# Fourier mixing on operands folded over tokens and channels, with the background tasks moved earlier

## The chip, the cores and the metric

The kernel runs on one core of one Trainium2 chip. Time is device microseconds (us) of one execution; the value used is the median of the runs. The core has the tensor engine (PE, with its weight loads as PEld), the vector engine (DVE), the scalar engine (ACT), GpSimd (POOL, idle here) and the queue that starts transfers (SP). Each engine works through its own instructions in a fixed order and waits on semaphores for the others.

## The reference

A two-layer backbone for 256 tokens `x` of 2048 channels and 256 context tokens `ctx`, all in fp32. Layer 0 multiplies the modulated, normed input by one wide matrix, feeds retention and Fourier mixing, gates both, and projects back. Layer 1 is a gated short convolution.

```python
def _fourier(u, fno_w):
    b, L, _ = u.shape
    ug = u.reshape(b, L, G_B, GB_DIM).astype(jnp.float32)
    f = jnp.fft.fft2(ug, axes=(1, 3), norm='ortho').real
    y = jnp.einsum('blgc,gcd->blgd', f.astype(u.dtype), fno_w)
    return y.reshape(b, L, B_WIDTH)
...
    qx, kx, vx, gax, ux, gbx = _split_even(hx @ w_in)
...
    yx = jnp.concatenate([_merge_heads(ret_x, hx.dtype) * jax.nn.silu(gax),
                          _fourier(ux, fno_w) * jax.nn.silu(gbx)], axis=-1) @ w_out
...
def _odd_layer(h, w_in, conv_w, w_out, rows):
    bg, cg, xt, g = jnp.split(h @ w_in, 4, axis=-1)
    y = bg * _conv3(cg * xt, conv_w, rows) * jax.nn.silu(g)
    return y @ w_out
```

Every layer starts with `rmsnorm(x) * (1 + scale) + shift` and ends with `x + gate * y`; scale, shift and gate are rows of `silu(c) @ ada_w + ada_b`. The Fourier part has 8 groups of 256 channels; the transform runs over the 256 tokens and the 256 channels of a group, and its real part is kept.

## The kernel before

Each fp32 operand is held as two parts, hi and lo, and a product is three matmul passes: hi by hi, lo by hi, hi by lo, summed in PSUM. All matmuls go through `mm` (L56). Activations lie channel-major: 8 tiles `hx` of 128 partitions x 2 x (256 hi | 256 lo), and 8 `hc` for the context.

A weight tile is 128x2048 fp32, 1 MB. SP loads it (`load_raw`, L82) into a ring `raw` of three buffers. `split_w` takes it in four quarters of 512: ACT casts the hi part (`whi`, L95), DVE subtracts it for the lo part (`wlo`, L59). Each of these rings has six quarters, so six quarters can be ready ahead of PE. `group_t` makes 256 output columns channel-major from two tiles (64 matmuls for one stream), `group_n` 512 columns token-major from four tiles (96 matmuls, 512 wide), and `group_d` sums the last block of a projection in one bank.

Two kinds of work are threaded through these groups. `bg` pops a background task at every second weight tile, unless `quiet` is set: a 1 MB load of a row block `adaT` into the same `raw` ring, and a DVE reduction with `scb` (L371) into a column of `gv`. There are 64 tasks; `finish_mods` adds a range of `gv` into `mods`, and first pops, one after the other, every task of that range that hasn't been popped. `hook` pops one closure from `stages` after every half weight tile; a closure holds a stage of a retention head (S, o, then the norm: sum `ss`, root on ACT, reciprocal on DVE at L190), or of a Fourier group. A scheduler then fixes the order on each engine.

The phases are: start (norms, first modulation); retention in four pairs `pr` of heads (K, Q, V, then two gates `gA`, ending in `yA`); Fourier mixing; output projection with `w0o` in eight blocks; layer 1 (`w1`, 64 groups); the second projection (`w1o`). Mixing has four rounds of one `group_n` for the product u (`gN`), a `fold` of u over the channel, and two gate groups. A Fourier group is `tables` (12 matmuls `pz` on the group's weights `wr`), `tokens` (18 matmuls `pP`) and `product` (12 matmuls `py`); then `gate` makes `yB`. Its `load` of `wr` goes into a buffer of its own, and is issued ahead of the groups of its round.

In the output projection `project` sets `quiet` for blocks 6 and 7. Of the 64 tasks 20 are popped in retention, 16 in mixing, 12 in the output projection, 16 in layer 1. At `finish_mods(16, 48)`, behind the projection, 48 have been popped. `modulate` then writes `h1` from `x1`: `modt` (L196), a cast, and `h` (L198).

## Time and profile before

| what | us |
|---|---|
| the three runs | 1835.57, 1834.95, 1835.39 |
| median | 1835.39 |
| span of the profiled execution | 1833.4 |
| matmuls (PE) busy | 1792.8 |
| DVE busy | 1202.4 |
| ACT busy | 906.0 |

The span is read from the first to the last instruction of one profiled execution; the runs' times lie 1.6 to 2.2 us above it, and no other time of that execution is given. A row of a group names line, engine, operation, output and input, shape and count, then busy time and mean nanoseconds of one, then the idle time before it and what ended it. A row of a window gives its length, the busy time of PE, PEld, DVE, ACT and POOL with the number of instructions, the granted PE clock (1.00 is full), the share of the DMA engines and GB/s. A row of the chain of waits gives start, duration, engine, tile, line and count. A row of an engine's timeline gives start, duration, engine, line, operation and, in brackets, the idle time ahead with what ended it. A row of the waits says who waited on whom: total, times, longest.

### The profile page before, as it was taken

The numbers are of one execution on the slowest core, as the hardware profiler recorded it, in microseconds if no ns is written. First come the engines' busy times: TensorE is split into PE (matmuls) and PEld (weight loads), VectorE is DVE, ScalarE is ACT, GpSimd is POOL, SyncE is SP. The second block draws the span as 40 slices with busy tenths as digits, with TensorE's granted clock in tenths as the row PEclk, the third lists the DMA queues.
The fourth block names the chain that finished last, engine by engine and source line by source line (L and its number), as shares of the span: only waits on it lengthen the run. The fifth ranks groups of instructions, "written<-read, shape, count | busy, mean of one in ns | idle before, by whom it ended". The sixth has DMA issues, their size and how long they took to land.

```text
span 1833.4 us, 26739 instructions
## 1 busy us (share of the span) xinstructions
PE 1792.8 (98%) x10200; PEld 1541.9 (84%) x10200; DVE 1202.4 (66%) x1862; ACT 906.0 (49%) x1491; POOL 0.2 (0%) x4
## 2 busy tenths in 40 slices
PE   5999999999999999999999999999999999999997
PEld 3667888888888888888978888888888888888887
DVE  5347747557477777777587888666666666665554
ACT  4225626345265554444555555555555555555553
POOL 0000000000000000000000000000000000000000
PEclk8999999999999999999999999999999999999999
DMA  9886445545466676777547877555555555555552
GB/s 389 327 319 246 144 156 184 180 165 186 150 238 250 243 258 229 262 291 287 196 161 253 299 279 288 191 187 197 191 184 191 196 188 185 189 199 186 186 192 105
DMA packets 58449, 400.87 MB, mean 219 GB/s; under 512 B 6480, under 2 KB 6608, under 8 KB 11088
## 3 DMA queue, kind: packets, MB, share of 16 engines
q1 hardware_dynamic: 58320, 399.16, 60.5%
q8 instruction: 80, 1.31, 0.3%
q14 instruction: 49, 0.40, 0.1%
HBM read 397.03 MB, written 2.10 MB: 218 GB/s over the span
## 4 chain that ended last, share of the span: by engine, by line
PE 95%; DVE 2%; ACT 1%; DMA 1%; issue 0%; SPq 0%; DVEq 0%
PE gT L56 70%; PE gN L56 12%; PE gD L56 3%; PE gemv L56 2%; PE pk L56 1%; PE o L56 1%; PE pvc L56 1%; PE pvx L56 1%; PE pP L56 1%; PE S L56 1%; PE pz L56 1%; PE py L56 1%; DMA raw<-w0s 1%; PE pq L56 1%; DMA xT<-xT 0%
## 5 line engine op out<-in xcount | busy, mean ns | idle before, releaser
L95 ACT CAST whi<-raw 128x512 fp32r<-128x512 f32 x1088 | 670.9, 622 | 746.1 <-PE gT L56 535.8
L59 DVE TENSOR_TENSOR wlo<-raw,whi 128x512 fp32r<-128x512 f32 x1088 | 738.3, 690 | 452.4 <-ACT whi L95 436.7
L56 PE MATMUL gT<-h,whi 128*128 128x512 f32 x2048 | 711.3, 392 | 4.2 <-DVE h L198 4.2
L56 PE MATMUL gT<-h,wlo 128*128 128x256 f32 x2048 | 573.2, 280 | 0.0
L56 PEld LDWEIGHTS gT<-h,whi 128*128 128x128 f32 x2048 | 383.6, 187 | 88.8 <-issue 4.5
L56 PEld LDWEIGHTS gT<-h,wlo 128*128 128x128 f32 x2048 | 387.5, 189 | 0.7 <-DVE wlo L59 0.3
L56 PE MATMUL gT<-hx,whi 128*128 128x512 f32 x704 | 254.5, 401 | 1.6 <-ACT v L478 1.6
L56 PE MATMUL gT<-hx,wlo 128*128 128x256 f32 x704 | 197.9, 281 | 0.1
L371 DVE CUSTOM_DVE_ANT_0 raw<-raw,scb 128x2048 f32<-128x2048 f32 x64 | 146.5, 2290 | 48.0 <-DMA raw<-adaT 45.0
L56 PEld LDWEIGHTS gT<-hx,whi 128*128 128x128 f32 x704 | 132.2, 188 | 32.3 <-ACT v L478 2.1
L56 PE MATMUL gT<-y,whi 128*128 128x512 f32 x448 | 155.3, 391 | 0.0
L56 PE MATMUL gN<-whi,hx 128*128 128x512 f32 x448 | 139.3, 392 | 0.0
L56 PEld LDWEIGHTS gT<-hx,wlo 128*128 128x128 f32 x704 | 132.9, 189 | 1.8 <-DVE wlo L59 0.7
L56 PE MATMUL gT<-y,wlo 128*128 128x256 f32 x448 | 125.4, 280 | 0.0
L56 PEld LDWEIGHTS gT<-y,whi 128*128 128x128 f32 x448 | 83.8, 187 | 18.4
L56 PEld LDWEIGHTS gN<-whi,hx 128*128 128x128 f32 x448 | 83.5, 188 | 16.9
L56 PE MATMUL gN<-wlo,hx 128*128 128x512 f32 x224 | 87.3, 390 | 0.0
L56 PEld LDWEIGHTS gT<-y,wlo 128*128 128x128 f32 x448 | 84.7, 189 | 0.0
L56 PE MATMUL gT<-yB,whi 128*128 128x512 f32 x224 | 79.5, 399 | 0.0
L56 PE MATMUL gT<-yA,whi 128*128 128x512 f32 x224 | 79.4, 398 | 0.0
L56 PE MATMUL gT<-yB,wlo 128*128 128x256 f32 x224 | 62.9, 281 | 0.0
L56 PE MATMUL gT<-yA,wlo 128*128 128x256 f32 x224 | 62.9, 281 | 0.0
(233 smaller groups left out, 1792.4 us busy)
## 6 DMA issues: line engine op xcount, KB each, us to landing
raw<-w SPq DMA_DIRECT2D x200, 1024.0 KB, 4.9
raw<-adaT SPq DMA_DIRECT2D x64, 1024.0 KB, 4.9
raw<-ada SPq DMA_DIRECT2D x32, 1024.0 KB, 6.9
raw<-w0o SPq DMA_DIRECT2D x32, 1024.0 KB, 4.9
raw<-w1o SPq DMA_DIRECT2D x32, 1024.0 KB, 4.8
raw<-w0s SPq DMA_DIRECT2D x8, 1024.0 KB, 5.7
xT<-xT SPq DMA_DIRECT2D x4, 512.0 KB, 6.7
cT<-ctxT SPq DMA_DIRECT2D x4, 512.0 KB, 16.2
```

The source lines that it names most:

```text
L56: nc.tensor.matmul(o, l, r, start=start, stop=stop, skip_group_check=True)
L59: nc.vector.tensor_tensor(o, x, hi.bitcast(F32), op=ALU.subtract)
L95: nc.scalar.copy(hi[:], sl)
L371: nc.vector.tensor_tensor_reduce(out=raw[:], in0=raw[:], in1=scb[:], scale=1.0, scalar=0.0, op0=ALU.mult, op1=ALU.add, accum_out=gv[:, j:j ...
```

## The change

Over tokens, `fold_x` makes sums and differences of tokens t and 256 - t from `hx` into new tiles `hf`, all eight in the last retention pair. Over channels, `half.fold` makes sums (`ef`) and differences (in place) of the columns c and 256 - c of the weights of u, two tiles per pair of 512 columns, before they are split. A cosine needs only the even sums and a sine only the odd differences, so each half of u (`u0`, `u1`; bank pair `pu`) takes 16 steps of 6 matmuls. What folding leaves over, token 128 and channel 128, goes through `uacc` (one DVE operation for each 512 columns), two fp32 products with `e0`, and `middle` (48 products 128x8 and one fp32). The gates are computed from `hf` and unfolded by `gate_unfold`.

The work is threaded anew: the 16 steps of `u0` hang on the gate groups 0 to 3, the steps of `u1` together with Fourier groups 0 to 3 on gate groups 4 to 7, and Fourier groups 4 to 7 on the first block of the output projection. The last pair of retention goes K, V, Q, gA. Background tasks come at every weight tile in the first three pairs (28), none from the last pair to the end of mixing, and at every second tile in the projection (12), so `finish_mods(16, 48)` pops eight. `wr` is loaded within `tables`, into a ring it shares.

```diff
+        often = [True]
...
-            if tasks and turn[0]:
+            if tasks and (turn[0] or often[0]):
...
+        hf = [None] * 8
+        xd = const.tile([P, 16], F32, name="xd")
+
+        def fold_x(e):
+            s = rp.tile([P, 2, 256], F32, tag="t2", bufs=5, name="hs")
+            add(s[:], hx[e][:, :, 0:256].bitcast(F32), hx[e][:, :, 256:512].bitcast(F32))
+            eo = rp.tile([P, 2, 256], F32, tag="t2", bufs=5, name="eo")
+            add(eo[:, :, 1:128], s[:, :, 1:128], s[:, :, 255:128:-1])
+            dif(eo[:, :, 129:256], s[:, :, 1:128], s[:, :, 255:128:-1])
+            add(eo[:, :, 0:1], s[:, :, 0:1], s[:, :, 128:129])
+            dif(eo[:, :, 128:129], s[:, :, 0:1], s[:, :, 128:129])
+            hf[e] = act_tile(f"c{e}", f"hf{e}")
+            split_act(hf[e], eo[:])
+            nc.vector.tensor_scalar(xd[:, 2 * e:2 * e + 2].unsqueeze(2), eo[:, :, 128:129], 2.0, None, op0=ALU.mult)
...
+            else:
+                quiet[0] = True
+                k, kc = keys()
+                keep(values())
+                stages += [(lambda e=e: fold_x(e)) for e in range(4)]
+                q = queries()
+                h0, h1 = heads()
+                stages += [h0[0], lambda: fold_x(4), h0[1], lambda: fold_x(5), h0[2], h1[0], lambda: fold_x(6), h1[1]]
...
+            if pr == 3:
+                fold_x(7)
+                h1[2]()
...
+        class half:
+            def __init__(self, hf):
+                self.hf, self.pu, self.raws = hf, None, {}
+            def fold(self, i):
+                raw = load_raw(a["w0u"][self.hf * 8 + i])
+                r = raw[:].rearrange("p (k s c) -> p k s c", k=2, s=2)
+                ef = fp.tile([P, 2, 512], F32, tag="ef", name="ef")
+                add(ef[:], r[:, :, 0, :], r[:, :, 1, :])
+                dif(r[:, :, 0, :], r[:, :, 0, :], r[:, :, 1, :])
+                if i == 0:
+                    self.acc = fp.tile([P, 512], F32, tag="acc", name="uacc")
+                self.raws[i] = (ef, r)
+            def step(self, kc):
+                if self.pu is None:
+                    self.pu = psum("pu")
+                    self.fold(0)
+                i, k2 = kc // 2, kc % 2
+                ef, r = self.raws[i]
+                w = []
+                for src in (ef[:, k2, :], r[:, k2, 0, :]):
+                    hi = wp.tile([P, 512], F32R, tag="whi", bufs=6, name="whi")
+                    lo = wp.tile([P, 512], F32R, tag="wlo", bufs=6, name="wlo")
+                    nc.scalar.copy(hi[:], src)
+                    sub(lo[:], src, hi[:])
+                    w.append((hi[:], lo[:]))
+                if kc == 0:
+                    nc.vector.tensor_scalar(self.acc[:], r[:, k2, 1, :], xd[:, 0:1], None, op0=ALU.mult)
+                else:
+                    nc.vector.scalar_tensor_tensor(self.acc[:], r[:, k2, 1, :], xd[:, kc:kc + 1], self.acc[:],
+                                                   op0=ALU.mult, op1=ALU.add)
+                x = hf[kc // 2]
+                for s in range(2):
+                    c0 = s * 128
+                    mm3(self.pu[:, s, :], (x[:, k2, c0:c0 + 128], x[:, k2, 256 + c0:384 + c0]), w[s], kc == 0,
+                        kc == 15 and s == 0)
+                if k2 and i < 7:
+                    self.fold(i + 1)
+                if kc == 15:
+                    mm(self.pu[:, 1, :], e0[:], self.acc[:], False, True)
+                    self.h = fp.tile([P, 2, 512], F32R, tag="uh", name="uh")
+                    self.l = fp.tile([P, 2, 512], F32R, tag="ul", name="ul")
+                    nc.scalar.copy(self.h[:], self.pu[:])
+                    sub(self.l[:], self.pu[:], self.h[:])
+                    for t in (self.h, self.l):
+                        t0 = t[:, 1, :].rearrange("p (g c) -> p g c", g=4)[:, :, 0:1]
+                        nc.vector.tensor_scalar(t0, t0.bitcast(F32), row0[:], None, op0=ALU.mult)
...
+                wr = fp.tile([P, 512], F32, tag="t2", bufs=4, name="wr")
+                nc.sync.dma_start(wr[:], a["fno"][g].rearrange("p a c -> p (a c)"))
+                wgh = wp.tile([P, 512], F32R, tag="whi", bufs=6, name="wgh")
+                wgl = wp.tile([P, 512], F32R, tag="wlo", bufs=6, name="wgl")
...
-                even, odd, mid = ubox[-1]
+                for t, src in zip(mids, (umh[:, g:g + 1], uml[:, g:g + 1], umh[:, 8 + g:9 + g], uml[:, 8 + g:9 + g])):
+                    nc.vector.tensor_copy(t[:, 0:1], src.bitcast(F32))
+                mh, ml, kh, kl = (t[:] for t in mids)
+                eh, el = u.h[:, 0, j:j + 128], u.l[:, 0, j:j + 128]
+                oh, ol = u.h[:, 1, j:j + 128], u.l[:, 1, j:j + 128]
                 pP = bank("pP")
-                for lc in range(2):
-                    i = 2 * lc + g % 2
-                    mm3(pP[:, 0:256], [t[:, i, :] for t in even],
-                        (th[:, lc, 0:256], tl[:, lc, 0:256]), lc == 0, lc == 1)
-                for lc in range(2):
-                    i = 2 * lc + g % 2
-                    mm3(pP[:, 256:512], [t[:, i, :] for t in odd],
-                        (th[:, lc, 256:512], tl[:, lc, 256:512]), lc == 0, False)
-                    mm3(pP[0:32, 256:512], [t[:, i, :] for t in mid],
-                        (th[:, lc, 0:256], tl[:, lc, 0:256]), False, lc == 1)
+                po = pP[:, 0:256]
+                mm3(po, (eh, el), (th[:, 0:256], tl[:, 0:256]), True, False)
+                mm(po, oh, nt[:], False, False)
+                mm(po, ol, nt[:], False, True)
+                po, p0 = pP[:, 256:512], pP[0:32, 256:512]
+                mm3(po, (oh, ol), (th[:, 256:512], tl[:, 256:512]), True, False)
+                mm3(p0, (mh, ml), (th[:, 0:256], tl[:, 0:256]), False, False)
+                mm(p0, kh, nt[:], False, False)
+                mm(p0, kl, nt[:], False, True)
...
-            def load():
-                wr = got["wr"] = fp.tile([P, 2, 256], F32, tag="wr", bufs=1, name="wr")
-                nc.sync.dma_start(wr[:], a["fno"][g])
...
-        for gp in range(4):
-            g0, g1 = fourier(2 * gp), fourier(2 * gp + 1)
-            g0[0]()
-            stages += [None, last, None, None, g0[1], None, None, None]
-            stages += [None, g0[2], None, g0[3], None, g1[1], g1[2], None]
-            pu, = group_n(w0, iw, [hx])
-            iw += 4
-            ubox.append(fold(pu))
-            g1[0]()
-            tg, = group_t(w0, iw, 2, [hx])
-            iw += 2
-            g0[4](silu_lr(fp, tg, "sgb", 1))
-            tg, = group_t(w0, iw, 2, [hx])
-            iw += 2
-            sgb = silu_lr(fp, tg, "sgb", 1)
-
-            def last(g1=g1, sgb=sgb):
-                g1[3]()
-                g1[4](sgb)
-        stages += [None, last]
...
+        def gate_unfold(g):
+            tg, = group_t(a["w0g"], 2 * g, 2, [hf])
+            s = lr(fp, tg, bufs=4, ring=4)
+            n = fp.tile([P, 2, 256], F32, tag="t2", bufs=4, name="un")
+            add(n[:, :, 0:128], s[:, :, 0:128], s[:, :, 128:256])
+            dif(n[:, :, 128:129], s[:, :, 0:1], s[:, :, 128:129])
+            dif(n[:, :, 129:256], s[:, :, 127:0:-1], s[:, :, 255:128:-1])
+            sgb[g] = fp.tile([P, 2, 256], F32, tag="sgb", bufs=4, name="sgb")
+            nc.scalar.activation(sgb[g][:], n[:], AF.Silu, scale=0.5)
...
+        stages += [(lambda kc=kc: u0.step(kc)) for kc in range(16)]
+        for g in range(4):
+            gate_unfold(g)
+        stages += [both(lambda kc=kc: u1.step(kc), *((middle,) if kc == 0 else ()), gs[kc // 4][kc % 4])
+                   for kc in range(16)]
+        for g in range(4, 8):
+            gate_unfold(g)
+        g4, g5, g6, g7 = gs[4:]
+        g4[0]()
+        g4[1]()
+        stages += [both(g4[2], g5[0], g5[1]), both(g4[3], g5[2], g6[0], g6[1]), both(g5[3], g6[2], g7[0], g7[1]),
+                   both(g6[3], g7[2]), g7[3]]
+        quiet[0] = often[0] = False
```

Three places show how the order moves. The first is PE at the end of retention; `ss` is the last head's sum of squares. Before, the first product for u follows it:

```order
L56 MATMUL gT_4003<-hx7_87,wlo_4084 128x256
L56 MATMUL ss_4119<-sq_4066,ones_72 128x256
L56 MATMUL gN_4168<-whi_4174,hx0_80 128x512 x2
L56 MATMUL gN_4168<-wlo_4175,hx0_80 128x512
L56 MATMUL gN_4168<-whi_4178,hx0_80 128x512 x2
```

In the changed kernel `gT_4300` is the first gate group of mixing, `o` the last head's weighted values:

```order
L56 MATMUL gT_4300<-hf3_3918,wlo_4316 128x256
L56 MATMUL o_4209<-mask_3317,v_3774 128x256 x6
L56 MATMUL ss_4238<-sq_4218,ones_72 128x256
L56 MATMUL pu_4335<-whi_4342,hf0_3819 128x512 x2
L56 MATMUL pu_4335<-wlo_4343,hf0_3819 128x512
L56 MATMUL pu_4335<-whi_4346,hf0_3819 128x512 x2
```

On DVE the changed kernel has these rows there, behind the reciprocal of that head, up to the first operations on a u weight tile (`eo`, `xd` and `hf7` belong to the last `fold_x`, `ot` and `yA7` to the head):

```order
L65 TENSOR_TENSOR eo_4229<-hs_4227 128x2
L68 TENSOR_TENSOR eo_4229<-hs_4227 128x2
L62 TENSOR_TENSOR ot_4243<-o_4209,rstd_4240 128x512
L467 TENSOR_SCALAR xd_1191<-eo_4229 128x2
L62 TENSOR_TENSOR ot_4243<-ot_4243,sga_4225 128x512
L59 TENSOR_TENSOR hf7_4234<-eo_4229,hf7_4234 128x2x256
L59 TENSOR_TENSOR yA7_4249<-ot_4243,yA7_4249 128x2x256
L559 MEMSET e0_4273 128x128
L562 MEMSET row0_4276 128x1
L566 MEMSET zero_4283 128x32
L65 TENSOR_TENSOR ef_4338<-raw_4336 128x1024
L637 TENSOR_SCALAR uacc_4341<-raw_4336,xd_1191 128x512
```

The head's last operations and the last `fold_x` now lie between `ss` and the first weights of u, on the engine that folds them.

The second place is SP at the end of mixing: `raw<-w0o` are weights of the output projection, `raw<-adaT` tasks, `wr` weights of a Fourier group.

```order
L85 DMA raw_5961<-w0g 128x2048
L675 DMA wr_5880<-fno 128x512
L85 DMA raw_6122<-w0o 128x2048
L85 DMA raw_6124<-adaT 128x2048
L85 DMA raw_6296<-w0o 128x2048
L85 DMA raw_6427<-w0o 128x2048
L675 DMA wr_6076<-fno 128x512
L675 DMA wr_6172<-fno 128x512
```

`wr_6076` is group 4's and `wr_6172` group 5's; the loads of groups 4 to 7 stand among those of the output projection, where before they all stood ahead of it.

The third place is SP and DVE at the boundary to layer 1. Before, on SP, from the last weights of the projection on (`xr` is a block of `x`):

```order
L82 DMA raw_7985<-w0o 128x2048
L82 DMA raw_8051<-w0o 128x2048
L685 DMA xr_7850<-xT 128x512
L82 DMA raw_8207<-w1 128x2048
L82 DMA raw_8257<-w1 128x2048
```

The changed kernel on SP:

```order
L85 DMA raw_8061<-w0o 128x2048
L813 DMA xr_7860<-xT 128x512
L85 DMA raw_8142<-adaT 128x2048
L85 DMA raw_8145<-adaT 128x2048
L85 DMA raw_8148<-adaT 128x2048
L85 DMA raw_8151<-adaT 128x2048
L85 DMA raw_8154<-adaT 128x2048
L85 DMA raw_8157<-adaT 128x2048
L85 DMA raw_8160<-adaT 128x2048
L85 DMA raw_8163<-adaT 128x2048
L85 DMA raw_8241<-w1 128x2048
```

And on DVE, where an `ISA` row on `raw` is a reduction (the first of the eight stands further up), `x1_7` the last block of the projection, and `rstd` its norm:

```order
L375 ISA raw_8151,gv_76<-raw_8151,scb_1185 128x2048
L375 ISA gv_76 128x1
L775 SCALAR_TENSOR_TENSOR x1_7_6547<-gD_7862,mods_77,xr_7860 128x256 x2
L375 ISA raw_8154,gv_76<-raw_8154,scb_1185 128x2048
L375 ISA gv_76 128x1
L194 RECIPROCAL rstd_8139<-rstd_8139 128x256
L375 ISA raw_8157,gv_76<-raw_8157,scb_1185 128x2048
L375 ISA gv_76 128x1
L375 ISA raw_8160,gv_76<-raw_8160,scb_1185 128x2048
L375 ISA gv_76 128x1
L375 ISA raw_8163,gv_76<-raw_8163,scb_1185 128x2048
```

The next DVE rows add `gv` into `mods`. Eight loads and eight reductions now stand between the projection and layer 1; before, the first `w1` load followed the projection's.

More of the change, by code (lines that the diff above doesn't have):

```diff
@@ new lines, in body, with mm3, middle @@
+        umh = fp.tile([P, 16], F32R, name="umh")
+        uml = fp.tile([P, 16], F32R, name="uml")
+        ys = yA + [None] * 8
+        def mm3(o, x, y, start, stop):
+            mm(o, x[0], y[0], start, False)
+            mm(o, x[1], y[0], False, False)
+            mm(o, x[0], y[1], False, stop)
+        def middle():
+            pm = bank("pm")
+            for kc in range(16):
+                x = hf[kc // 2]
+                mm3(pm[:, 0:8], (x[:, kc % 2, 0:128], x[:, kc % 2, 256:384]), (dmh[:, kc, :], dml[:, kc, :]),
+                    kc == 0, kc == 15)
+            pr = fp.tile([P, 16, 8], F32, tag="t2", bufs=4, name="pr")
+            mul(pr[:], dm[:], xd[:].unsqueeze(2).to_broadcast([P, 16, 8]))
+            cr = fp.tile([P, 8], F32, name="cr")
+            nc.vector.tensor_reduce(cr[:], pr[:].rearrange("p k g -> p g k"), axis=AX.X, op=ALU.add)
+            nc.vector.tensor_scalar(cr[:], cr[:], 0.5, None, op0=ALU.mult)
+            mm(pm[:, 8:16], e0[:], cr[:], True, True)
+            nc.scalar.copy(umf[:], pm[:, 0:16])
+            nc.scalar.copy(umh[:], umf[:])
+            sub(uml[:], umf[:], umh[:])
@@ new lines, in body, with both, f @@
+        u0, u1 = half(0), half(1)
+        gs = [fourier(g, u0 if g < 4 else u1) for g in range(8)]
+        def both(*fs):
+            def f():
+                for x in fs:
+                    x()
+            return f
+        stages += [(lambda kc=kc: u0.step(kc)) for kc in range(16)]
[5 more added lines that the diff above has]
+            gate_unfold(g)
@@ L692, in body @@
                                        op0=ALU.add, op1=ALU.mult)
[L695 removed]
+        h1 = [act_tile(f"c{e}", f"h1_{e}") for e in range(8)]
         for kc in range(16):
```

182 lines of the change are left out of this document (95 added, 87 removed).

## The prediction

> **What bounds the kernel now.** I read the page's head first, then the mean durations of the two splitting steps, then the stretch in which the change works (windows from 500 to 800 us).
>
> ```profile
> span 1833.4 us, 26739 instructions
> PE 1792.8 (98%) x10200; PEld 1541.9 (84%) x10200; DVE 1202.4 (66%) x1862; ACT 906.0 (49%) x1491; POOL 0.2 (0%) x4
> PE 95%; DVE 2%; ACT 1%; DMA 1%; issue 0%; SPq 0%; DVEq 0%
> ```
> ```profile
> 500.00:600.00 100.00, 100.00 (x541) 86.61 (x540) 76.73 (x113) 57.05 (x95) 0.00 (x0) 1.00 0.68 253
> 600.00:700.00 100.00, 100.00 (x573) 87.55 (x572) 72.70 (x105) 52.41 (x91) 0.00 (x0) 1.00 0.65 238
> 700.00:800.00 100.00, 100.00 (x583) 87.66 (x582) 72.20 (x104) 49.28 (x84) 0.00 (x0) 1.00 0.70 264
> ```
> ```profile
> L59 DVE TENSOR_TENSOR wlo<-raw,whi 128x512 fp32r<-128x512 f32 x1088 | 738.3, 690 | 452.4 <-ACT whi L95 436.7 <-PE gT L56 1.3
> L371 DVE CUSTOM_DVE_ANT_0 raw<-raw,scb 128x2048 f32<-128x2048 f32 x64 | 146.5, 2290 | 48.0 <-DMA raw<-adaT 45.0 <-ACT scb L366 2.7
> L95 ACT CAST whi<-raw 128x512 fp32r<-128x512 f32 x1088 | 670.9, 622 | 746.1 <-PE gT L56 535.8 <-PE gN L56 113.7 <-DVE wlo L59 36.5
> ```
>
> The tensor engine (PE) is busy in all of each of the three windows, at clock 1.00, and 95% of the chain that ended last is PE. The casts on ACT wait for PE (535.8 us), not PE for them. So a matmul taken out saves its time in full, and nothing else saves anything, as long as PE stays fed. The engine nearest to the bound is DVE: 72 to 77% there. The question of this change is what PE loses in waits where it now has 98%.
>
> **What is removed and added on PE.** These pieces of the chain of waits give start, duration and count; the last row is from PE's timeline.
>
> ```profile
> 238.18 1.73 PE S L56 x8
> ...
> 518.90 5.55 PE gT L56 x32
> 524.45 0.43 PE ss L56 x2
> 524.88 21.79 PE gN L56 x96
> ...
> 681.76 2.13 PE pP L56 x18
> ```
> ```profile
> 142.49 0.95 PE L56 MATMUL gemv<-cols,gs 128*128 128x2 f32 x8
> ```
>
> A matmul 512 wide takes 21.79/96 = 0.227 us. The u product falls from 4 x 96 = 384 of them to 192: -43.6. The token transforms fall from 18 to 13 per group at 2.13/18 = 0.118, 40 in all: -4.7. The middle channel's 48 products 128x8 have no row. Their floor is that row's 0.95/8 = 0.119, their ceiling a 512-wide 0.227; so narrow, they lie at the floor: +5.7 (to 10.9). The products of e0 are plain fp32, as ss is: that one instruction, 256 wide, shows as two passes of together 0.43 (S has 1.73/8 a pass as well), so two that are 512 wide take 0.87 each, and a narrow one 0.12: +1.9. The gates keep 64 matmuls a group. PE's work changes by -48.3 + 7.6 = **-40.7**.
>
> **The mixing phases.** Durations of DVE operations overlap, so I count from start to start:
>
> ```profile
> 516.62 0.69 DVE L59 TENSOR_TENSOR wlo<-raw,whi 128x512 fp32r<-128x512 f32 x1
> 517.23 0.68 DVE L62 TENSOR_TENSOR ot<-o,rstd 128x512 f32<-128x512 f32 x1
> ...
> 527.35 1.75 DVE L190 RECIPROCAL rstd<-rstd 128x256 f32<-128x256 f32 x1 [0.98 <-ACT rstd L189]
> 529.01 0.63 DVE L59 TENSOR_TENSOR wlo<-raw,whi 128x512 fp32r<-128x512 f32 x1
> ```
> ```profile
> L65 DVE TENSOR_TENSOR nacc<-nacc,sq 128x1024 f32<-128x1024 f32 x6 | 7.3, 1224 | 8.5 <-ACT sq L240 8.5
> ```
>
> An operation of 512 starts 0.61 after the one before (517.23 - 516.62) though it is recorded for 0.69; a reciprocal holds DVE 1.66; one of 1024 I take as 1.14 (1.224 less the same 0.08). In the first half a u tile and a gate tile together give DVE two folds of 1.14, eight weight subtracts (4.88), two accumulations (1.3; a row of 512 says 0.61 at least) and half a gate's sum and unfolding (0.6): 9.1 us. PE has 12 x 0.227 + 5.65 = 8.4 in that pair, and 0.7 of the narrow products: 9.1. In the second half a group of the transform adds on average 37 x 0.118 / 2 = 2.2 on PE and five operations of 512 with small copies, 3.4/2 = 1.7, on DVE: 10.6 against 10.8. DVE goes from 73% to about level with PE, though 16 reductions have left these phases. Two engines at level, in order, with rings of six quarters between them, never fit exactly: +6, between 1 (the queues absorb it) and 13 (9% of some 145 us).
>
> The Trainium skill, in "VectorE: DVE Perf Modes", section "The DRAIN you can't avoid", has the next vector operation wait until the pipe has emptied, and adds that one which is not held starts earlier. By that rule the phase would go as in the second rival; the starts 0.61 apart under records of 0.69 speak for its exception.
>
> **The entry into mixing.** In the changed order the last head's S, o and ss stand behind only the first gate tile, and ss is followed on PE by the first u matmul. Before, a block of 96 weight matmuls, whose operands were long ready, stood there. On DVE the first fold `ef` stands behind the head's whole tail. From ss's end (524.88) the row above has the reciprocal 2.47 later; then 1.66; the last fold_x in four pieces, 0.7; ot twice, hf7 and yA7 at 0.61, 2.4, with 0.35 for ACT's cast; memsets and xd 0.4; ef 1.14; the cast 0.62. PE stands for 9.7. Behind it DVE still has the second fold, four accumulations, tables and ten subtracts before the second tile's first u operands are ready: about 14 us from the first u matmul, and PE has 9.5 to do: 4.3 more. **+14** (10 if the catch-up is hidden, 17 if table casts on ACT come between).
>
> **Retention.** Tasks go from 20 in 40 tiles to 28 in 28, so in one-stream tiles SP moves 2 MB per 5.65 us, 371 GB/s.
>
> ```profile
> 40.00:50.00 10.00, 9.58 (x54) 6.81 (x54) 5.68 (x14) 3.54 (x8) 0.00 (x0) 0.83 1.01 421
> DVE raw L371 <- DMA raw<-adaT: 45.0, 33, 4.1
> raw<-adaT SPq DMA_DIRECT2D x64, 1024.0 KB, 4.9
> ```
>
> 421 GB/s has been reached at the start, so it fits; DVE too, with 4 x 0.61 + 2.2 in 5.65. But a reduction holds DVE while its transfer is late (45.0 us in 33 waits, up to 4.1), and the next tile's quarters queue behind it. Most of such waits are covered by the six quarters, worth 8 us of PE. +3, from 0 to 8 (half a us in each of 16 one-stream tiles).
>
> **The end of mixing.** SP issues `wr` of group 4 behind an output weight load that waits for a task's reduction; before, it stood a group earlier, in a buffer of its own. After the last e0 matmul PE's next is that group's pz, whose wgh stands on ACT behind uh, a yB cast, a silu with its table, and itself:
>
> ```profile
> L522 ACT COPY uf<-gN 128x1024 f32<-128x1024 f32 x4 | 4.0, 1010 | 0.0
> L189 ACT ACT_TABLE_LOAD x8 | 10.3, 1283 | 0.1
> ```
>
> 1.0 + 0.6 + 1.3 + 0.6 + 0.6 = 4.2, or 4.9 for the transfer less what PE still had. Four groups then share bank and operand slots with the first output weights; for these I add 3: **+7** (4 to 13).
>
> **The layer boundary.** Only 28 + 12 tasks are done, and 48 are asked for, so eight loads stand on SP ahead of the first w1 load, and eight reductions on DVE. Rows of before, from SP's and DVE's timeline and the chain:
>
> ```profile
> 904.85 17.61 SPq L82 DMA_DIRECT2D raw<-w  x4
> 923.76 0.88 DVE L647 SCALAR_TENSOR_TENSOR x<-gD,mods,xr 128x256 f32<-128x256 f32 x2 [0.21 <-PE gD L56]
> ```
> ```profile
> 926.42 1.76 DVE rstd L190
> 928.21 1.28 DVE modt L196 x3
> 929.49 0.41 DVE h L198
> 930.03 30.04 PE gT L56 x162
> ```
> ```profile
> 930.00:935.00 5.00, 4.97 (x21) 4.36 (x22) 5.00 (x13) 3.60 (x9) 0.00 (x0) 0.71 0.00 0
> ```
>
> The first reductions hide behind the last block. The fourth ends near 925.9, as the ring's slots come free with that block's last quarters (8 us ahead of its end), and x1 stands behind it, 2.1 late. Then x1 (0.9), four reductions at 2.2 (2.29 less 0.08) and the reciprocal: 937.3. Adding the reduced rows into the modulation columns 0.5, and modt to the first matmul 1.8, gives 939.6; the w1 tile gets its slot when the third last reduction ends (932.9), lands 4.9 later, is cast and waits for h's casts: 941. PE starts 11 later than at 930.03, without prepared quarters, and DVE then has sixteen modulations beside the subtracts: **+13** (9 to 16). No quarter of w1 is prepared in that gap, so what covered the old one of 4.2 us is gone.
>
> After the old gap the clock was 0.71: 21 matmuls took 4.97 where 21 x 0.177 = 3.7, a loss of 1.3. Two new gaps (entry, end of mixing): +2 (0 to 4).
>
> **Sum.** -40.7 + 6 + 14 + 3 + 7 + 13 + 2 = +4.3. The profiled span of 1833.4 becomes 1837.7; the runs (median 1835.39) lie 2.0 above it: **1839.7**. The unknown costs at their lower ends give 24 of waits, -16.7; at their upper ends with 5.2 more for the narrow products, 71 and 5, +35, but they don't all fall one way; half of it, +17, is where I stop.
>
> **Rivals.**
> - *The ring hides what is not a chain.* PE waits only where results depend on each other: entry 9.7, boundary 10, end 4, the rest nothing: -40.7 + 24 = -17, 1818.7. For it: DVE at 77% cost PE nothing between 500 and 600. Against it: there the subtracts were idle 452 us in all, waiting for ACT; in the new phases there is no such slack. It decides from 37 us of waits downwards (-3.67). Chance 0.25.
> - *DVE becomes the bound.* If an operation cost its recorded 0.69 and not 0.61, DVE would have some 13% more in 145 us of mixing, +18 beyond the forecast: 1857.7. It speaks against it that starts are 0.61 apart. Chance 0.12.
> - *Loads bind in retention.* Each of the 16 one-stream tiles waits 0.5 more than the ring covers: +8 in place of 3, and more where two-stream tiles follow: 1845 to 1850. The 421 GB/s speaks against it, the 33 waits for it. Chance 0.08.
> - *The change does not shorten the u product*, because each weight tile must still be loaded, folded and split: at old pace, it would be over 1860. The balance above excludes most of it; it is in DVE's chance.
>
> **How the numbers follow.** The forecast with its own 1832 to 1849 has 0.55. A measurement of this kernel can tell some 0.2% (3.67 us) from no change: 1831.7 to 1839.1. The forecast lies at the upper edge, so its 0.55 is 0.27 within and 0.28 above. Faster 0.25 (first rival), same 0.27, slower 0.28 + 0.12 + 0.08 = 0.48. The range of 1822 to 1854 leaves out some 0.2: the first rival's lower part and most of DVE's.
>
> **What would show it.** A gap of PE near 515 to 530 of about 10 us before the first pu matmul; PE at 93 to 97% through the mixing, with DVE over 90%; a gap before pz of the fifth group with wgh or wr as releaser; eight reductions in one row at the boundary, with h1's first matmul some 17 us after gD's last, 11 more than before; retention still at 100%. It would be wrong if the mixing windows show PE at 99%, or the gap at entry under 6, or if new waits appear in layer 1, whose order I took as unchanged.

## The result, and the profile after

| what | before | after |
|---|---|---|
| runs (us) | 1834.33 to 1835.57 | 1845.95, 1848.65, 1849.31, 1851.78 |
| median | 1835.17 | 1848.98 |
| ratio of the times | | 1.0076, 95% interval 1.0061 to 1.009 |
| span of the profiled execution | 1833.4 | 1844.1 (of the run of 1845.95) |
| matmuls (PE) busy | 1792.8 | 1761.7 |
| first matmul of layer 1 | 930.0 | 939.0 |

The kernel became slower by 13.8 us. The forecast of 1839.7 lies 9.3 below. First the head of the page of the changed kernel and its chain by engine:

```profile
span 1844.1 us, 26501 instructions
PE 1761.7 (96%) x10022; PEld 1506.7 (82%) x10022; DVE 1271.0 (69%) x2034; ACT 895.6 (49%) x1484; POOL 0.2 (0%) x4
PE 90%; DVE 4%; DMA 3%; ACT 1%; issue 1%; SPq 0%; DVEq 0%; ACTq 0%
```

PE is busy for 31.1 us less, as meant, and the span is 10.7 longer: 41.8 us of PE standing still are new. The windows tell where. All that end at 125 to 525 us are the same in both kernels, but for 0.1 us, so retention lost nothing. Windows of the changed kernel behind it (length, busy PE, PEld, DVE, ACT and POOL, granted clock, share of DMA, GB/s):

```profile
525.00:550.00 25.00, 13.40 (x40) 8.91 (x39) 21.68 (x44) 11.83 (x21) 0.00 (x0) 0.66 0.26 82
...
575.00:600.00 25.00, 25.00 (x134) 21.36 (x133) 24.97 (x42) 14.93 (x26) 0.00 (x0) 1.00 0.60 214
600.00:625.00 25.00, 23.45 (x125) 19.44 (x124) 23.23 (x41) 14.69 (x27) 0.00 (x0) 1.00 0.61 226
625.00:650.00 25.00, 21.63 (x121) 17.91 (x121) 22.75 (x43) 11.57 (x21) 0.00 (x0) 0.96 0.48 170
650.00:675.00 25.00, 24.48 (x142) 21.30 (x142) 23.10 (x44) 14.20 (x26) 0.00 (x0) 0.98 0.55 197
675.00:700.00 25.00, 23.16 (x136) 20.12 (x135) 23.35 (x40) 11.96 (x22) 0.00 (x0) 1.00 0.55 201
700.00:725.00 25.00, 18.88 (x102) 16.20 (x101) 17.75 (x31) 8.78 (x15) 0.00 (x0) 0.86 0.53 189
725.00:750.00 25.00, 21.23 (x132) 18.43 (x131) 13.54 (x31) 10.42 (x19) 0.00 (x0) 0.93 0.32 111
900.00:950.00 50.00, 32.28 (x217) 29.69 (x217) 42.74 (x65) 19.34 (x38) 0.00 (x0) 0.80 0.73 275
```

The last of these windows in the kernel before:

```profile
900.00:950.00 50.00, 45.69 (x309) 41.94 (x309) 36.51 (x69) 28.71 (x52) 0.00 (x0) 0.97 0.48 162
```

PE stands for 11.6 us at the entry (25 less 13.40), 7.3 from 600 to 700, 9.9 from 700 to 750, and 17.7 at the boundary where it stood 4.3 before. In the columns of the clock is what the idle time brought along: 0.66, 0.86 and 0.80 around the same places. What ended PE's waits in mixing (who waits on whom: us, times, longest), in the changed kernel:

```profile
PE pz L56 <- ACT wgh L678: 11.8, 4, 6.1
PE pu L56 <- ACT whi L633: 8.4, 2, 8.1
PE gT L56 <- ACT whi L98: 4.8, 4, 2.8
PE pu L56 <- DVE wlo L59: 1.2, 1, 1.2
PE ss L56 <- DVE sq L65: 1.2, 1, 1.2
```

`pz` needs `wgh`, the hi part of `wr`: four waits of 11.8 us in all. The chain of waits (start, duration, what) says why, at the end of mixing:

```profile
700.91 4.86 DMA raw<-adaT
...
705.90 2.29 DVE raw L375
...
708.20 0.60 DVE yf L62
708.80 0.61 DVE t L65
...
709.43 4.70 DMA wr<-fno
...
714.21 0.63 ACT wgh L678
...
717.99 4.69 DMA raw<-adaT
...
722.81 2.29 DVE raw L375
...
725.51 6.32 DMA wr<-fno
```

A task's transfer and its reduction stand in front of the operation that frees a buffer of the ring `t2`; the load of `wr` waits for that buffer, and SP, in order, issues nothing behind it meanwhile. In the second turn, within 31 us, `wr` stands on SP behind an output weight load (issued at 725.14) that waits for the buffer of the task's own reduction.

### The profile page after: what moved, and what is told of

Same layout as the page of the kernel before. It is cut to its first block, busy times and chain, and to the rows that moved or that the text cites. A ratio compares the mean times of both kernels' runs of the same rounds, so it can differ in the third digit from the quotient of the medians.

```text
span 1844.1 us, 26501 instructions
## 1 busy us (share of the span) xinstructions
PE 1761.7 (96%) x10022; PEld 1506.7 (82%) x10022; DVE 1271.0 (69%) x2034; ACT 895.6 (49%) x1484; POOL 0.2 (0%) x4
## 4 chain that ended last, share of the span: by engine, by line
PE 90%; DVE 4%; DMA 3%; ACT 1%; issue 1%; SPq 0%; DVEq 0%; ACTq 0%
PE gT L56 69%; PE gN L56 7%; PE gD L56 2%; PE gemv L56 2%; PE pu L56 2%; PE o L56 1%; DMA raw<-adaT 1%; PE pvx L56 1%; PE pk L56 1%; PE pvc L56 1%; DVE wlo L59 1%; DMA wr<-fno 1%; PE S L56 1%; PE pq L56 1%; DVE raw L375 1%
## 5 line engine op out<-in xcount | busy, mean ns | idle before, releaser
L59 DVE TENSOR_TENSOR wlo<-raw,whi 128x512 fp32r<-128x512 f32 x1056 | 714.7, 689 | 376.6 <-ACT whi L98 355.3
L98 ACT CAST whi<-raw 128x512 fp32r<-128x512 f32 x1024 | 626.8, 620 | 690.2 <-PE gT L56 512.1
L56 PE MATMUL gT<-h,whi 128*128 128x512 f32 x2048 | 712.6, 395 | 15.6 <-DVE h L202 15.0
L56 PE MATMUL gT<-hx,whi 128*128 128x512 f32 x448 | 161.6, 399 | 1.6 <-ACT v L493 1.6
L56 PE MATMUL gT<-hx,wlo 128*128 128x256 f32 x448 | 126.5, 282 | 0.0
L56 PEld LDWEIGHTS gT<-hx,whi 128*128 128x128 f32 x448 | 83.9, 188 | 21.2 <-ACT v L493 2.1
L56 PE MATMUL gT<-hf,whi 128*128 128x512 f32 x256 | 93.2, 400 | 1.7 <-ACT whi L98 1.7
L56 PEld LDWEIGHTS gT<-hx,wlo 128*128 128x128 f32 x448 | 84.6, 189 | 1.2 <-DVE wlo L59 0.5
L56 PE MATMUL gT<-hf,wlo 128*128 128x256 f32 x256 | 73.2, 286 | 0.3 <-DVE wlo L59 0.2
L185 ACT COPY lr_r<-gT 128x512 f32<-128x512 f32 x103 | 59.9, 581 | 7.3 <-PE gT L56 7.2
```

Source lines behind the costliest of these rows:

```text
L56: nc.tensor.matmul(o, l, r, start=start, stop=stop, skip_group_check=True)
L59: nc.vector.tensor_tensor(o, x, hi.bitcast(F32), op=ALU.subtract)
L98: nc.scalar.copy(hi[:], sl)
L185: nc.scalar.copy(r[:], t[:, :, 256:512])
```

## The experiments

What the theories have to tell apart: whether the time is lost in a few waits, each with its own cause and a slower clock behind it (theory 1), or in DVE being level with PE through all of mixing, so that a wait removed only shows the next (theory 2). Where not told otherwise, "less" is against the changed kernel's 1848.98.

### e1_spread: the tasks of the boundary into the output projection

```diff
                 quiet[0] = b >= 6
+                often[0] = 2 <= b < 6
```

> The eight tasks of the boundary go into blocks 2 to 5 of the output projection, one at every weight tile there; nothing else changes. Theory 1 (the waits cost their idle time, and the clock that drops behind each gap costs more on top): between 900 and 950 us PE's idle time falls from 17.7 us to the 4.3 that it had before, and with the clock there back from 0.61 to some 0.93 another 2.6 us go; the time falls by about 16, to 1833. Theory 2 (the work of the eight tasks costs its time wherever it stands, since a tile and a task together are 2 MB per 5.65 us): PE waits in blocks 2 to 5 instead, the windows from 790 to 880 us are no longer full, and the time falls by 8 at most, to 1841 or more.

Measured 1840.82 (1836.76 to 1857.37 in ten runs, two of them at 1854.75 and above): 8.2 less, ratio to the kernel before 1.0038 (1.0008 to 1.0068). Its windows over the projection and the boundary:

```profile
800.00:850.00 50.00, 47.94 (x270) 40.77 (x269) 40.41 (x57) 19.60 (x36) 0.00 (x0) 1.00 0.92 339
850.00:900.00 50.00, 49.27 (x278) 42.04 (x277) 40.45 (x59) 23.04 (x41) 0.00 (x0) 1.00 0.90 340
900.00:950.00 50.00, 45.69 (x309) 41.97 (x309) 35.70 (x66) 28.33 (x51) 0.00 (x0) 0.97 0.44 154
```

The boundary is that of the kernel before again, 45.69 busy at 0.97. But PE stands 2.8 us in the blocks that got the tasks, at 340 GB/s, and the same matmuls lose more than that: from the start of the projection's long piece in the chain (770.67, in the changed kernel 766.95) to its last block (906.47 against 896.87) they take 5.9 us longer. Both theories have a share: the burst was on the path, as layer 1 now starts 29.3 us behind the start of the last block instead of 42.1, and a task at every one-stream tile isn't free either. The 3.7 us by which this execution is late already at the start of that piece have nothing to do with the edit: up to there PE's matmuls are the same in the same order, and the difference lies in the clock (shown in the section on the prediction).

### e2_wr: the channel weights in buffers of their own

```diff
+            def load():
+                wr = got["wr"] = acts.tile([P, 2, 512], F32, tag=f"hx{6 + g % 2}", name="wr")[:, 0, :]
+                nc.sync.dma_start(wr, a["fno"][g].rearrange("p a c -> p (a c)"))
+
             def tables():
-                wr = fp.tile([P, 512], F32, tag="t2", bufs=4, name="wr")
-                nc.sync.dma_start(wr[:], a["fno"][g].rearrange("p a c -> p (a c)"))
+                wr = got["wr"]
...
                 got["z"] = split_bank(pz, "z")
+                if g < 6:
+                    gs[g + 2][4]()
```

> The channel weights wr of a Fourier group get two buffers of their own (in the tiles hx6 and hx7, free by then) and are loaded two groups ahead, no longer in the ring t2. Theory 1 (the transform waits for these late transfers): PE's waits for wgh, 11.8 us in four, vanish, the idle time between 700 and 750 us falls from 9.9 to under 3, the clock there goes up again, and the time falls by about 13, to 1836. Theory 2 (DVE is the bound of the whole mixing, wr only the last of its late results): the waits turn into waits for wlo or whi of the same length, and the time falls by 3 at most, to 1846.

Measured 1831.41 (1829.66 to 1834.23): 17.6 less, and under the kernel before, ratio 0.9982 (0.9972 to 0.9991). No wait for `wgh` is left, and the windows from 700 to 750 are full at clock 1.00:

```profile
650.00:675.00 25.00, 23.61 (x140) 20.38 (x138) 25.00 (x50) 14.22 (x25) 0.00 (x0) 1.00 0.59 201
675.00:700.00 25.00, 24.68 (x143) 21.20 (x142) 25.00 (x43) 13.69 (x26) 0.00 (x0) 1.00 0.62 215
700.00:725.00 25.00, 25.00 (x157) 22.14 (x157) 21.46 (x38) 14.29 (x24) 0.00 (x0) 1.00 0.70 243
725.00:750.00 25.00, 25.00 (x171) 22.91 (x170) 19.50 (x35) 11.97 (x21) 0.00 (x0) 1.00 0.49 179
```

Theory 1 holds. The profiled executions differ by 13.6 (spans of 1830.5 and 1844.1): the idle time from 600 to 750 fell by 13.2 and the loss to the clock by 5, but the gap ahead of layer 1 is now 16.9 instead of 15.0, and the output projection ran at 0.1766 us a matmul instead of 0.1734 (last section). The edit gives `wr` other buffers and also loads it two groups ahead, so the runs don't tell which of the two is needed. What is left shows DVE at 25.00 of 25 from 650 to 700: behind the late loads the second theory's bound does seem to exist, at a much lower price; `e13_noacc` looks at it.

### e3_entry: the first steps of u two hooks later

```diff
-        stages += [(lambda kc=kc: u0.step(kc)) for kc in range(16)]
+        s0 = [(lambda kc=kc: u0.step(kc)) for kc in range(16)]
+        stages += [None, None, s0[0], s0[1], both(s0[2], s0[3])] + s0[4:9] + [both(s0[9], s0[10])] + s0[11:]
```

> The steps of u0 start two hooks later, so that most of the first gate group's 64 matmuls stand ahead of the first u matmul, and the last head's tail and the first fold lie beside them. Theory 1: the gap of 8.06 us ahead of the first u matmul shrinks by some 5.6 to 2.5, with less of the slow clock behind it (4.6 us of loss between 525 and 550): the time falls by 7 to 9, to 1841. Theory 2 (DVE is the bound behind the entry): PE loses in the next gate groups what it gains at the entry, and the time falls by 2 at most.

Measured 1857.46 (1856.71 to 1859.17): 8.5 more, which neither theory had. The entry is not where it comes from: the first matmul of layer 1 starts at 935.4 instead of 939.0, so up to there 3.6 us are won (the wait ahead of `pu` is gone, but the first gate group now waits 5.1 us for the last `hf`). It is lost in layer 1, whose code is the same. The long piece of the chain in this kernel:

```profile
943.32 876.87 PE gT L56 x4963
```

The same piece in the changed kernel, without the edit:

```profile
946.67 861.51 PE gT L56 x4968
```

A matmul takes 0.1767 here and 0.1734 there, over 5,000 of them 16 us, with PE never idle and the granted clock 1.00 in both. That is the subject of the last section; the experiment shows 3.6 us for the entry, not 7 to 9, and this from one execution of each kernel, while two executions of the same matmuls can differ by 3.7 through the clock alone.

### e8_all: the three edits together

> The three edits together. Theory 1: their gains add up, 16 + 13 + 8 = 37, to about 1812, 23 us under the kernel before. Theory 2 (DVE bounds the mixing): only the boundary's 13 to 16 come, and some of the entry: 1830 to 1835.

Measured 1833.98 (1832.01 to 1841.29, ratio 1.000, 0.9991 to 1.001). Layer 1 starts at 918.9, 20.1 earlier than in the changed kernel and 11.1 earlier than before. In the profiled execution (1841.29) layer 1 then runs at the lower rate, 884.64 us for 4992 matmuls, 0.1772 each; how the nine others ran there isn't known. The sum of 37 isn't reached: by themselves the entry gave less than half of its share and the spreading half, and together they don't even add up to that, as PE stands 4.5 us from 800 to 850 (45.49 of 50 busy), where `e1_spread` had 2.1.

### e5_warm: PE kept busy at the boundary

```diff
                         mm(tot[:, 0:256], ones[:], sq[:, m, :], False, m == 1)
+                    if post is None:
+                        keep = bank("keep")
+                        for i in range(52):
+                            mm(keep[:], ys[0][:, 0, 0:128], ys[0][:, 0, :], True, True)
```

> The changed kernel with 52 idle matmuls 128x512 on PE behind the last sum of the projection, whose result nobody reads: PE is busy in the gap at the boundary, while everything it waits for there (eight reductions, modulations) is as it was. Theory 1 (the clock drops because PE stood, and the rate behind the gap follows the clock): the 52 matmuls take some 12 to 20 of the 15 us, the first matmuls of layer 1 then run at clock 1.00 with 0.35 us for a pair from the start, where they took 0.64 for the first 2.5 to 3 us, so that some 2 us are won between the first matmul of layer 1 and the 100th. Theory 2 (the slow start comes from DVE and ACT, which prepare quarters and h behind the gap): the pairs stay at 0.64 or wait for h and wlo as before.

One run, 1867.84. The idle matmuls didn't fill the gap. Eighteen of them went ahead of the last sum, which made everything behind it later (layer 1 starts at 945.3, 6.3 later than in the changed kernel, of which 3.7 were lost in mixing before), and after the others PE stood for 5.75 us. Behind that gap PE's timeline reads as behind the gap of the changed kernel:

```profile
945.28 0.77 PE L56 MATMUL gT<-h,whi 128*128 128x512 f32 x1 [5.75 <-DVE h L202]
...
946.06 0.63 PE L56 MATMUL gT<-h,whi 128*128 128x512 f32 x1
...
949.23 0.39 PE L56 MATMUL gT<-h,whi 128*128 128x512 f32 x1
...
949.58 0.39 PE L56 MATMUL gT<-h,whi 128*128 128x512 f32 x1
```

Pairs start 0.64 to 0.78 us apart for four microseconds and 0.35 apart from 949.23 on. A gap of 5.75 is enough for the low clock, and the experiment says nothing on a boundary without one; its question stays open. (Layer 1 ran at the lower rate here as well, 0.1767.)

### e6_burst_before: the burst alone, in the kernel before

```diff
         for gp in range(4):
+            quiet[0] = gp >= 2
...
         stages += [None, last]
+        quiet[0] = False
```

> The kernel before, with one thing of the change alone: no tasks in the second half of mixing (8 fewer), so that eight are popped at the layer boundary. Theory 1 (the burst is on the path, whatever the rest does): the first matmul of layer 1 comes 9 to 13 us later than at 930.03, and the time rises by 10 to 16, to 1845 to 1851. Theory 2 (the burst only hurts because DVE is late from mixing): under 4 us, below 1839.

Measured 1863.75 (1863.47 to 1866.55), 29.1 above the kernel before, ratio 1.0162 (1.0148 to 1.0177). The boundary and the long piece behind it:

```profile
900.00:950.00 50.00, 32.28 (x224) 29.62 (x223) 42.97 (x65) 19.17 (x36) 0.00 (x0) 0.83 0.74 271
```
```profile
948.30 877.20 PE gT L56 x4964
```

PE is busy for 32.28 of 50 us, to the hundredth as in the changed kernel, and layer 1 starts at 940.7, 10.7 late. So the burst alone makes the boundary of the changed kernel, as theory 1 had it. The time missed its 1845 to 1851, because another 14.8 us come from the lower rate in layer 1 (877.20/4964 less 867.31/4992, times 4992); some 3.6 remain, for the slow start among others.

### e9_pr3 and e10_pr3_wr: the eight tasks in the last retention pair

```diff
             if tasks and (turn[0] or often[0]):
                 tasks.pop(0)()
+                quiet[0] = len(tasks) == 28
...
-                quiet[0] = True
                 k, kc = keys()
```

> The changed kernel, with the eight tasks of the boundary at the first eight weight tiles of the last retention pair, where the trace of the changed kernel has 85 to 120 GB/s and DVE at 30 to 65%. Theory 1: the gap at the boundary is 4.2 us again, and PE loses nothing in blocks 2 to 5 of the projection, where it lost 2.8 with the tasks there: the first matmul of layer 1 comes 13 us earlier than at 938.98, at 926, and the time falls by 13 to 16, to 1833 to 1836. Theory 2 (DVE is late at the entry for any work put ahead of it): the first u matmul comes later than 537.2 by some us, and the time falls by 8 at most.

Measured 1834.80 (1831.26 to 1836.09): 14.2 less, ratio to the kernel before 0.9998 (0.9989 to 1.0007). Layer 1 starts at 928.2. The projection is undisturbed, and the boundary that of the kernel before:

```profile
800.00:850.00 50.00, 50.00 (x290) 43.73 (x289) 37.85 (x54) 24.61 (x40) 0.00 (x0) 1.00 0.77 286
850.00:900.00 50.00, 50.00 (x294) 43.88 (x293) 31.84 (x50) 25.08 (x41) 0.00 (x0) 1.00 0.67 244
900.00:950.00 50.00, 45.69 (x302) 41.97 (x301) 36.37 (x69) 28.56 (x52) 0.00 (x0) 0.93 0.44 157
```

With `wr` in its own buffers besides:

> Both edits, the eight tasks in the last retention pair and wr in buffers of its own: theory 1 has the first matmul of layer 1 at 913 (925.67 with wr alone, less 13), and the time at 1816 to 1819, 16 to 19 us under the kernel before. Theory 2 (PE has a lower steady rate in layer 1 in some kernels, 0.1767 us a matmul instead of 0.1735, as two of the runs so far showed at full granted clock, and a shorter time up to there doesn't decide it): up to 17 us come back in layer 1, and the time is 1830 to 1836.

Measured 1816.95 (five runs from 1814.50 to 1817.26, two at 1831.8), ratio 0.9922 (0.9895 to 0.995). The gains add up: 17.6 + 14.2 = 31.8, measured 32.0. Layer 1 starts at 911.4. The two runs at 1831.8 lie 15 above the rest, as much as theory 2 named, but only one of the five others was profiled, at the higher rate.

### e11_heads: the last head earlier

```diff
-                stages += [h0[0], lambda: fold_x(4), h0[1], lambda: fold_x(5), h0[2], h1[0], lambda: fold_x(6), h1[1]]
+                stages += [both(h0[0], lambda: fold_x(4)), h1[0], both(h0[1], lambda: fold_x(5)), h0[2],
+                           both(h1[1], lambda: fold_x(6)), h1[2], lambda: fold_x(7), None]
```

> The kernel with the eight tasks in the last retention pair and wr in its own buffers (1816.95), and the second head of the last pair started two stages earlier, its norm and the last fold on the last gate group. Theory 1 (the entry is a chain from the last o to the first u weight, and what is taken out of it comes back): with o, its square and part of the folds beside the last gate group, the idle time in 525 to 550 us falls from 11.5 to 8 or 9 and the time by 2 to 4, to 1813 to 1815. Theory 2 (DVE in front of the entry has no room for it, everything on it arrives as late as before): the first u matmul stays at 538 or later, and the time doesn't fall.

Measured 1815.56 (1814.61 to 1816.59), ratio to the kernel before 0.9896 (0.9881 to 0.9911). That is 1.4 under the kernel without this edit, but within the spread of its five lower runs; layer 1 starts at 910.8 instead of 911.4. The first u matmul comes as late as without the edit (538.23), out of a wait as long as the old ones together:

```profile
538.31 1.22 PE L56 MATMUL pu<-whi,hf 128*128 128x512 f32 x2 [9.27 <-ACT whi L637]
```

The second theory is right here: `o` stands earlier on PE, but the reciprocal still starts at 530.41 (530.72 without the edit). The last `hf` then comes earlier (532.68 instead of 534.53), and yet the fold of the first weights starts at 536.36 (536.28), behind the head's `yA`, ahead of which DVE now waits 0.68 for ACT's cast.

### e13_noacc: 30 DVE operations out of mixing

```diff
-                else:
-                    nc.vector.scalar_tensor_tensor(self.acc[:], r[:, k2, 1, :], xd[:, kc:kc + 1], self.acc[:],
-                                                   op0=ALU.mult, op1=ALU.add)
```

> The same kernel (1816.95) without the accumulation for token 128 over the 512 columns, so that uacc has only the first of 16 terms: 30 operations of DVE less, 0.66 us each, 20 in all, out of mixing, where DVE was busy in 24.8 to 25.0 of 25 us from 625 to 700. Theory 1 (with wr early, DVE is what is left as the bound of mixing): the idle time of PE between 600 and 700, 3.8 us, falls under 1, some of the catching up behind the entry goes too, and the time falls by 3 to 6. Theory 2 (the rest are waits of the chain at the entry and of single loads): it falls by less than 1.5.

This kernel leaves out 15 of the 16 terms for token 128 in each half of u, so it tells about time alone. Measured 1822.92 (1822.34 to 1824.64), 6.0 over e10_pr3_wr where 3 to 6 less were expected, again by the rate in layer 1 (875.52 us for 4955 matmuls, 0.1767). Up to the first matmul of layer 1 it is 9.5 us faster, 901.9 against 911.4, and mixing from 550 to 750 has no idle time of PE:

```profile
575.00:600.00 25.00, 25.00 (x136) 21.41 (x135) 22.74 (x37) 15.41 (x28) 0.00 (x0) 1.00 0.69 246
650.00:675.00 25.00, 25.00 (x151) 22.14 (x150) 22.92 (x40) 15.34 (x29) 0.00 (x0) 1.00 0.65 221
```

Some 20 us of DVE taken away (30 operations at about 0.66) gave 8.8 of PE behind the first u matmul, which itself came 0.7 earlier (537.48 against 538.23): once `wr` is early, what is left in mixing hangs on these operations. They hold DVE and they also read the weights' `raw` buffers, and the run doesn't separate the two.

## Why the prediction was right, and what it missed

The direction, the forecast case and the places were right. By its terms, with the profiled executions (span +10.7):

| term | predicted | measured | from |
|---|---|---|---|
| work of PE | -40.7 | -42.8 | busy -31.1, less 11.7 for the clock |
| retention | +3 | 0 | windows up to 525 |
| entry, idle | +14 | +11.6 | window 525 to 550 |
| mixing phases, idle | +6 | +7.3 | windows 600 to 700 |
| end of mixing, idle | +7 | +9.9 | windows 700 to 750 |
| boundary, idle | +13 | +13.4 | 17.7 less 4.3 |
| clock | +2 | +11.7 | PE busy in slices of 1 us, times 1 less the clock |

The measured terms make +11.1; -0.4 is spread over other places. All but the clock together came 3 us lower than forecast, the clock 9.7 higher.

**The step that failed is the clock.** The prediction took "21 matmuls took 4.97 where 21 x 0.177 = 3.7, a loss of 1.3" from the one old gap and "Two new gaps (entry, end of mixing): +2". Counted over slices of 1 us, PE lost 4.6 us to a clock under 1.00 at the entry, 5.7 in mixing and 2.9 at the boundary, 13.2 where the kernel before lost 1.5. The mechanism was right, the size wrong by a factor of six. The clock changes on a grid of frames of 3.41 us, by how busy PE was in the frame (worked out in the last section). These are frames of the changed kernel behind the entry:

```profile
538.55:541.96 3.41, 1.96 (x3) 0.79 (x3) 3.41 (x7) 2.36 (x5) 0.00 (x0) 0.50 0.11 39
541.96:545.37 3.41, 2.62 (x7) 1.87 (x7) 3.41 (x7) 2.10 (x5) 0.00 (x0) 0.50 0.23 50
545.37:548.79 3.42, 3.42 (x11) 2.74 (x11) 3.42 (x5) 0.62 (x1) 0.00 (x0) 0.50 0.62 256
548.79:552.20 3.41, 3.41 (x22) 2.94 (x20) 3.41 (x7) 1.76 (x3) 0.00 (x0) 1.00 0.85 308
```

The old gap ended with operands ready for PE; PE was busy for 2.90 of 3.41 us in the one frame at half, and the clock was back within 3 us. At the entry PE starts again at 537.2 into small waits (for wlo, whi, dmh), is busy for 1.96 and 2.62 us of the next two frames, and stays at 0.50 until behind the first full frame, at 548.8, for 11.6 us. In mixing the late loads bring three more stretches at half, from 647.8, 712.6 and 733.1 on. The Trainium skill, in "TensorE: Matmul & The Clock Gate", section "What's actually happening", has the clock halved by an idle window of about 3.4 us and restored only by about as long a time of sustained work. The 0.50, the length of a frame and the way back agree; that the whole window must be idle does not, as a frame in which PE was busy for 42% was enough (`e1_spread`, last section). The prediction priced the gap, but not the way PE comes out of it, nor the short gaps that fill half a frame.

The size also differs between executions. `e1_spread` and `e5_warm` run the changed kernel's matmuls in its order up to 800 us, and yet reach the projection's long piece 3.7 us later (770.67 and 770.69 against 766.95), with PE's idle time from 525 to 750 the same to 0.3 us and its loss to the clock 4.0 higher: a frame at 0.50 from 607.8 on that the changed kernel's profile doesn't have, and two from 648.8 on where it has one.

**The phases and the end of mixing** came to 17.2 us of idle time, 13 were forecast, and the share of their causes was wrong, so that 7.3 from 600 to 700 came near the forecast 6 is partly luck. The prediction gave 6 to DVE being level with PE, and 7 to "wr of group 4 behind an output weight load that waits for a task's reduction". Such a wait exists: it is the second turn of the chain shown above, for group 6, while the load of group 4, in the first turn, waited for a buffer of `t2` behind a reduction on DVE. But the loads of groups 1 to 3, inside the phases, came late too: SP held that of group 1 for 4.5 us for a buffer of `t2`, and those of groups 2 and 3 stood behind weight loads that waited up to 5.0 for a buffer of `raw`. PE's waits for `wgh` are 3.3, 0.5, 1.8 and 6.1 us in groups 1 to 4. `e2_wr` took 17.6 us away with these loads; some 4 us of idle time were left between 600 and 700, which `e13_noacc` removed by taking operations from DVE.

**The boundary**: eight reductions in a row, 13.4 us of idle time more, against +13 (which had some clock in it). `e6_burst_before` makes the same window in the kernel before, and `e9_pr3`, with the tasks elsewhere, removes it. The chain there goes three times through a load (4.98, 6.22 and 6.16 us) and a reduction (2.29) in turn, each load waiting for the buffer that the reduction frees, so the loads weigh more than the reductions by which the prediction counted the time. **The entry**: the gap from `ss` to the first u matmul was 8.06, where 9.7 was forecast, and another 1.21 came ahead of `ss`; the 4.3 for catching up came mostly as slow clock. The reciprocal starts 0.55 behind `ss` (529.72 after 529.17), not the 2.47 that the prediction read from the kernel before. `e3_entry` won 3.6 up to layer 1 and `e11_heads` 0.6, so how much of the entry can be had is not shown. **Retention** held, at 28 tasks in 28 tiles, as its lower end had it.

**The work on PE**: -42.8 against -40.7. Before, 864 matmuls of the output projection took 152.64 us, 0.1767 each; now 749 took 129.91, 0.1734 each. Over a stretch of 864 that is 2.8, the difference and something over; the terms beside it miss both ways (at full clock the 48 narrow products took 0.094 each instead of 0.119, those of u 0.236 instead of 0.227). What sets the rate isn't known (last section), so that the sum came this near is partly luck.

**Of the rivals**, the first (the ring hides all but chains) fell with the 41.8 us of new waits. The second has its mechanism in part, since mixing hangs on DVE's operations when `wr` is early, but not its price or reason: DVE's operations of 512 still start 0.60 to 0.61 apart under records of 0.68. The third fell with retention at no loss, and the fourth with PE's 42.8 us less. The terms for the profiled execution, which was the fastest of four, explain 10.7 of the 13.8; the other three runs took 2.7 to 5.8 longer than it at a mean clock of 0.977 to 0.981 against 0.982, and were not profiled; the 3.7 us by the clock in `e1_spread` and `e5_warm` are of that size.

The change as such is worth having. With two of its side effects undone it takes 1816.95 instead of 1835, and 1815.56 with the third edit; so a little under half of the 40.7 us that were to be taken from PE is kept there.

## What to carry to other kernels

Taking work from the bound engine pays only as far as the other engines' lookahead allows: ask for every removed stretch which loads and preparations had been hidden beside it, and for every small load whose buffers it waits for, since an in-order queue behind it waits too. Price an idle gap of PE with the slow clock behind it, and this by what PE finds when it starts again: a start into further waits cost three times one with all operands ready here (4.6 us against 1.5). Background work that is merely put off until it is due comes back as a burst at the worst place; put it where the trace shows both the queue and the engine free.

## What the runs showed of the hardware

**Two steady rates at full clock.** In layer 1 the same alternating matmuls (512 and 256 wide) run for 860 us without a pause, granted clock 1.00, DMA at 190 GB/s, at 0.1734 to 0.1739 us each (the upper figures hold the slow start) in some profiled executions (before, after, e1_spread, e2_wr, e9_pr3, e10_pr3_wr, e11_heads) and at 0.1767 to 0.1772 in others (e3_entry, e5_warm, e6_burst_before, e8_all, e13_noacc). The group of its first product shows it, here in the changed kernel:

```profile
L56 PE MATMUL gT<-h,whi 128*128 128x512 f32 x2048 | 712.6, 395 | 15.6 <-DVE h L202 15.0 <-ACT whi L98 0.6
```

And in e3_entry, with an almost equal wait ahead:

```profile
L56 PE MATMUL gT<-h,whi 128*128 128x512 f32 x2048 | 725.7, 400 | 16.1 <-DVE h L202 15.9
```

Over the stretch that makes 15 to 17 us, more than the whole change. All four runs of e3_entry, of e6_burst_before and of e13_noacc lie within 3.1 us of each other, so a kernel seems to keep to one rate; but two of seven runs of e10_pr3_wr are 15 higher, two of ten of e1_spread 14 and 17 above its median, and one of 25 of the kernel before, at 1851.01, 16; none of these was profiled. An execution doesn't keep to one rate: the output projection ran at 0.1767 in the kernel before, whose layer 1 ran at 0.1737, and at 0.1734 (129.91/749) in e3_entry, whose layer 1 ran at 0.1767. What chooses the rate is open: the code of layer 1 is the same in all of these, neither the length of the gap ahead (4.2 or 15 us) nor the time of its start orders them, and no experiment was made on it. Where kernels are compared, times up to the first matmul of layer 1 are free of layer 1's share of it; the projection's is under 3 us (0.0033 for each of 864 matmuls).

**The clock goes by frames, not by gaps.** In every trace the stretches at 0.50 begin and end on a grid of 3.41 us that runs through the whole execution; in the changed kernel they start at 531.72, 647.78, 712.63, 733.11 and 924.26 and last 5, 1, 2, 1 and 6 frames. What PE did in a frame decides the next. Over the twelve traces, from 500 to 960 us: of the frames at full clock, all 41 with PE busy under 46% were followed by one at 0.50, none of those busy over 55%, and two of six between. Of the frames at 0.50, all 40 busy over 95% were followed by full clock, none of the 65 under 84%, and three of seven between. Two frames at full clock with the ones behind them, in e1_spread and in e5_warm:

```profile
604.38:607.79 3.41, 1.44 (x7) 1.04 (x8) 1.68 (x2) 2.33 (x5) 0.00 (x0) 1.00 0.54 226
607.79:611.21 3.42, 3.42 (x13) 2.85 (x12) 3.42 (x7) 1.45 (x3) 0.00 (x0) 0.50 0.27 38
```
```profile
925.27:928.68 3.41, 2.15 (x9) 1.80 (x10) 2.01 (x5) 0.81 (x2) 0.00 (x0) 1.00 1.08 356
928.68:932.10 3.42, 3.42 (x17) 2.84 (x16) 2.91 (x3) 0.29 (x1) 0.00 (x0) 1.00 0.89 335
```

In the first the gap was 2.30 us long and PE busy for 42%; in the second 2.04 us and 63%, and the eighteen idle matmuls behind it took 4.38, 0.24 each, near the 0.227 of full clock. So a gap's length alone doesn't tell its price: the same 4.15 us ahead of layer 1 were followed by one frame at 0.50 in the kernel before and by two in e9_pr3, and PE lost 1.5 us in the one and 2.6 in the other.
